# Turning the queries of A and both sides of B's and C's heads through memory, on Trainium2

## The chip, the cores and the metric

The kernel runs on one core of a Trainium2 chip. The metric is the device time of one execution in microseconds (us). TensorE (PE in the profile) multiplies matrices, VectorE (DVE), ScalarE (ACT) and GpSimd (POOL) work on tiles in the core's memory (SBUF; VectorE and ScalarE also on PSUM, where TensorE writes), and SyncE (SP) issues most of the DMAs. Each engine works through its own instructions in order and waits on semaphores.

## The reference, cut to what matters

Two layers of a decoder trunk over 256 tokens of width 1024, all in float32. Each layer is a feed-forward half step, a mixer, and another feed-forward half step. The mixer projects the tokens once and splits the result among three groups of attention heads of width 64:

```python
proj = u @ w_in
aq = apply_rope(rms_norm(aq, a_q_norm), cos, sin)       # A: 4 query heads
ak = apply_rope(rms_norm(ak, a_k_norm), cos, sin)       #    1 shared key head
o_a = dsa_attention(aq, ak, av, iq, ik, iw)             #    keys chosen per query by an indexer, top 64
bq = apply_rope(rms_norm(bq, b_q_norm), cos, sin)       # B: 4 heads, one causal block of 256
bk = apply_rope(rms_norm(bk, b_k_norm), cos, sin)
o_b = moba_attention(bq, bk, bv)
cq, ck = rms_norm(cq, c_q_norm), rms_norm(ck, c_k_norm) # C: 8 heads, no rotation
log_f = log_sigmoid(cf + forget_bias)
o_c = forgetting_attention(cq, ck, cv, log_f) * sigmoid(cg)
return concat([o_a, o_b, o_c]) @ w_out
```

Scores are products over the 64 columns of a head. TensorE sums over partitions, so queries and keys, which the projection leaves with tokens in partitions, have to be turned: columns of two heads to 128 partitions, tokens along the row.

## The kernel before

**Weights.** All weights stream through once. A raw piece of 512 KB is loaded by SP (`Weights.issue`, `load`, L214) into one of ten buffers, ScalarE rounds it (`high`, L273, tile `wh`) and VectorE takes the rest (`low`, L277, tile `wl`), into one of eight pairs; TensorE multiplies with both parts (L383). `W.pump` makes the next pair. `W.hold` stops new loads, `W.free` lets them go on.

**The mixer** (`mixer`). The projection goes over 32 weight units; a unit is a *step*: twelve matmuls, then `run_side`, then a pump. The chunks come in this order: the indexer's queries and small things with B's queries (steps 1 to 8), B's keys and values (9 to 12), A (13 to 16), C's keys (17 to 20), C's queries (21 to 24), C's values (25 to 28), C's gate (29 to 32). After a chunk's last unit its `post_` function empties PSUM and books later work with `at_step(number, fn)`; `run_side` issues what is due at the end of a step, in order of the numbers. So an instruction's place on each engine is set by such numbers, and the engines run as far ahead as their waits let them.

**Turning.** `pairs_T` (L986, L988) turns a pair of heads by transposes on TensorE into a PSUM bank, which ScalarE copies: `bq_turn` and `bk_turn` at step 18.83, `a_turn` at 26.29. C's 16 transposes come after step 32 in `c_T` (L1444, L1445), one pair of heads of queries and keys each, into the tile `spare`. The kernel has another way already, for the feed-forward's hidden tiles, the gate and one pair of probabilities: `to_memory` transposes 32x32 blocks on VectorE (L474, STREAM_TRANSPOSE) and writes them to DRAM (L475), `from_memory` reads them back in four DMAs (L479), so that the blocks come out in their places. `blocks` joins the two.

**Norms.** The heads' norm factors come from ScalarE's squares, VectorE's sums (L963) and a power on GpSimd (`rsqrt`, L394); GpSimd multiplies by them (`scale_heads`, L955), rotates (`rope`, L947 to L950) and applies C's gains `gc` (L1236). `c_norm` does both sides of C at step 25.36.

**Attention.** `run_heads` gives functions for scores, masks (m), exponentials (e), divisions (d on VectorE, D on ScalarE) and flips (f: the transposes of the probabilities on TensorE, L1318). B's are booked by step. After step 32, `AC_ORDER` lists the words for A's heads (0 to 3) and C's (4 to 11) with the output projection's halves (q) among them; `s` are scores of a pair of heads, `g` is `c_T`, `a` adds the causal mask to a pair of C's forget rows on GpSimd (L1145). So m0, e0, D0, f0 are the first head of A. A's mask `amask` is made on VectorE (L1099 to L1103) after the last pass of the top-8 selection (L1092, L1094). C's forget rows are written to DRAM by ScalarE's queue and spread over the partitions from there (`mask_tiles` at step 29.63).

Of the kernel before, what the change touches and what calls it, by code (L numbers as in the profile page):

```python
# [18 lines left out]
P = 128  # L19
S = 256  # L20
# [19 lines left out]
g2.4 g0.5 s0.01 m0 s1.23 m3 e0 e3 s2.45 D0 q g1.0 a0 m4 m2 e2 q q D3 f0.3 a1 a3 m1 e1 s3.42 s4.01 f3.3  # L40
m5 e4 a2 m6 d2 q g3.5 d1 f2.3 q e5 m7 f1.5 m8 D4 s5.32 t m10 v0.0 w o0 e10 q q q e6 f4.3 q d5 m11 d10
# [5 lines left out]
B_TURN, A_ROPE, B_STEP, A_ROOT, A_TURN, SUMS_STEP, MASK_STEP = 18.83, 19.48, 20.73, 23.66, 26.29, 22.33, 29.63  # L47
# [248 lines left out]
def kernel(ctx: ExitStack, tc: tile.TileContext, x, xt, weights, small, const, out):  # L296
# [625 lines left out]
    def mixer(l, norm, nxt):  # L922
        room = wide().rearrange("p (n h d) -> p n h d", n=4, h=8)
# [90 lines left out]
        def post_ib(ps):  # L1014
# [132 lines left out]
        def post_a(ps):  # L1147
# [80 lines left out]

        def post_ck(ps):
            c_sums(0, ck, ps, 20.76)  # L1230

        def post_cq(ps):
            c_sums(1, cq, ps, 24.83)
            for t in range(2):
                q = cq[t]
                G.tensor_tensor(q, q, gc[:, None, :].to_broadcast([P, 8, HD]), op=ALU.mult)  # L1236

            def c_norm():
                rs = head_rs(c_ss.rearrange("p i t h -> p (i t h)"), 32, "c")
                for t in range(2):  # L1240
                    for i, d in enumerate((ck, cq)):
                        x = d[t]
                        scale_heads(x, x, rs[:, 16 * i + 8 * t:16 * i + 8 * t + 8])

            at_step(25.36, c_norm)
# [20 lines left out]
        def run_heads(hs, qk, take, emit=None):
            pj, pt, op, sums, bs = {}, {}, {}, {}, {}

            def scores(i):

                kind, h = hs[i]
                if h % 2:
                    return
                q, k = qk(kind, h)
                bs[i], bs[i + 1] = take(), take()
                for cols, qs, ks in ((slice(0, P), slice(0, P), slice(0, P)),
                                     (slice(P, 3 * P), slice(P, S), slice(0, S))):
                    products((bs[i], bs[i + 1]), cols, q[:, qs], k[:, ks], cols.start == 0)
# [45 lines left out]
            def flip_pair(i):  # L1324

                d = tab.rearrange("p a b t d -> p (a b t d)")[:, :6 * P]
                blocks([pj.pop(2 * i + e) for e in range(2)], 3, "pd", d.rearrange("p (i x) -> p i x", i=8))
# [98 lines left out]
        cT = st["cT"]  # L1426

# [11 lines left out]
        def c_T(j, copy):  # L1439

            b = take()
            for c, src in enumerate((cq, ck)):
                for t in range(2):
                    T.transpose(b[:, c * S + t * P:c * S + (t + 1) * P], src[t][:, 2 * j:2 * j + 2], ident)  # L1444
            copy(cT[:, j], b.rearrange("p (c s) -> p c s", c=2))  # L1445

        def blocks(tiles, n, name, to):
            sc = memory(n, name)
            for t, x in enumerate(tiles):
                to_memory(sc, t, x, n)  # L1450
            from_memory(sc, to, nc.sync)

        def turn_gate(_):
            blocks(st["gate"], 4, "gd", st["sg"].rearrange("p i m r -> p i (m r)"))

        def qk_ac(kind, h):
            if kind == "A":
                return st["aqT"][:, h // 2], st["akT"][:, 0]
            return cT[:, h // 2, 0], cT[:, h // 2, 1]
# [3 lines left out]
        run = dict(q=lambda i: next(halves), w=lambda i: W.pump(), m=masks, e=exps, d=divide, D=lambda i: divide(i, True),  # L1463
                   T=flip_pair, t=turn_gate,
                   s=lambda i: scores(2 * i), f=flip, F=lambda i: flip(i, V.tensor_copy),
                   g=lambda i: c_T(i, A.copy), G=lambda i: c_T(i, V.tensor_copy),
# [70 lines left out]
```

## Time and profile before

| | us |
|---|---|
| median of 3 runs (lowest to highest) | 975.02 (974.76 to 975.63) |
| the profiled execution | 974.23 |
| its span, first to last instruction | 972.5 |
| TensorE busy in the span | 967.3 |
| VectorE busy in the span | 822.5 |
| ScalarE busy in the span | 611.1 |
| GpSimd busy in the span | 167.2 |

Names such as `ps_gu<-wh,xhl` are the tile written and the tiles read. A duration of a matmul includes its way through the array, so rows of matmuls overlap; what one costs on the path is read from the chain or from the starts of its neighbours. "[0.50 <-PE ps_gu L383]" at a row's end says that the engine sat idle for 0.50 us before it, until TensorE's write.

### The profile page before, as it was taken

To read this page: it belongs to the slowest core of one execution; us is meant where nothing else is said; L and a number is where in the kernel's file an instruction comes from. 1 tells how busy PE (TensorE), PEld (TensorE's weight loads), DVE (VectorE), ACT (ScalarE), POOL (GpSimd) and SP (SyncE) were. 2 spreads that over 40 slices of the span, in tenths; PEclk is the share of its full clock that TensorE was granted. 3 is DMA by queue.
4 is the path that set the end of the run, shared out by engine and by line. 5 is a ranking of instruction groups with operands and counts; after the bars stand their busy time and mean duration, and the time that the engine had idled before them with its cause. 6 is when DMAs were issued, how large, how long until landed. Compare 5 with 4: busy or idle time off the path is not lost.

```text
span 972.5 us, 13771 instructions
## 1 busy us (share of the span) xinstructions
PE 967.3 (99%) x4608; PEld 801.1 (82%) x4608; DVE 822.5 (85%) x1284; ACT 611.1 (63%) x1024; POOL 167.2 (17%) x190
## 2 busy tenths in 40 slices
PE   9999999999999999999999999999999999999998
PEld 8888888888878888888878888888888788888887
DVE  6999698789987799879679987977899877998794
ACT  7756574567876656537475654756677966575562
POOL 0000002187630000000000000031867200000000
PEclk9999999999999999999999999999999999999999
DMA  9878877685555686769587777867657447687661
GB/s 360 309 198 335 281 257 217 210 295 170 184 183 161 249 229 240 268 193 315 174 322 267 209 248 246 289 197 255 245 160 232 167 147 268 186 304 265 183 243 65
DMA packets 105495, 226.68 MB, mean 233 GB/s; under 512 B 20928, under 2 KB 50896, under 8 KB 105424
## 3 DMA queue, kind: packets, MB, share of 16 engines
q1 hardware_dynamic: 101936, 213.95, 63.2%
q0 software_dynamic: 2304, 8.39, 4.9%
q10 hardware_dynamic: 1184, 3.46, 1.1%
q8 instruction: 36, 0.59, 0.2%
q14 instruction: 35, 0.29, 0.1%
HBM read 208.44 MB, written 17.33 MB: 232 GB/s over the span
## 4 chain that ended last, share of the span: by engine, by line
PE 97%; DMA 2%; DVE 1%; SPq 0%; ACT 0%; issue 0%; POOL 0%; ACTq 0%; POOLq 0%
PE ps_gu L383 65%; PE ps_acc L383 29%; PE ps_gu L1318 1%; PE ps_acc L986 1%; DMA xd<-tmp 1%; PE ps_acc L418 0%; DMA hd<-tmp 0%; DMA hT<-hd 0%; PE ps_acc L1318 0%; DMA xT<-xd 0%; PE ps_acc L1444 0%; SPq L479 0%; DVE tmp L474 0%; DVE trunk L490 0%; DVE wl L277 0%
## 5 line engine op out<-in xcount | busy, mean ns | idle before, releaser
L383 PE MATMUL ps_gu<-wh,xhl 128*128 128x512 f32 (+2 forms) x1600 | 493.7, 386 | 0.6 <-ACT xhl L447 0.6
L277 DVE TENSOR_TENSOR wl<-raw,wh 128x1024 fp32r<-128x1024 f32 (+2 forms) x340 | 405.1, 1228 | 13.4 <-ACT wh L273 13.3
L273 ACT CAST wh<-raw 128x1024 fp32r<-128x1024 f32 (+2 forms) x340 | 340.0, 1040 | 55.1 <-PE ps_gu L383 16.9
L383 PEld LDWEIGHTS ps_gu<-wh,xhl 128*128 128x128 f32 x1600 | 298.8, 188 | 59.3 <-ACT xhl L447 1.1
L383 PE MATMUL ps_gu<-wl,xhl 128*128 128x512 f32 (+2 forms) x800 | 305.9, 384 | 0.0
L383 PEld LDWEIGHTS ps_gu<-wl,xhl 128*128 128x128 f32 x800 | 150.3, 188 | 28.1
L383 PE MATMUL ps_acc<-wh,hh 128*128 128x512 f32 (+1 forms) x352 | 136.8, 389 | 0.2 <-ACT hh L567 0.2
L383 PE MATMUL ps_acc<-wh,hl 128*128 128x512 f32 (+1 forms) x352 | 136.7, 388 | 0.0
L383 PE MATMUL ps_acc<-wl,hh 128*128 128x512 f32 (+1 forms) x352 | 136.4, 387 | 0.0
L273 ACT CAST wh<-wide 128x1024 fp32r<-128x1024 f32 x48 | 50.2, 1054 | 85.7 <-DVE wide L244 55.1
L242 POOL DMA_DIRECT2D raw<-in_weights_dram x16 | 14.3, 893 | 377.3 <-DVE wide L244 256.0
L383 PEld LDWEIGHTS ps_acc<-wh,hl 128*128 128x128 f32 x352 | 66.1, 188 | 14.7 <-DVE hl L568 1.4
L383 PEld LDWEIGHTS ps_acc<-wh,hh 128*128 128x128 f32 x352 | 66.1, 188 | 14.0 <-ACT hh L567 0.9
L383 PEld LDWEIGHTS ps_acc<-wl,hh 128*128 128x128 f32 x352 | 66.1, 188 | 13.5
L277 DVE TENSOR_TENSOR wl<-wide,wh 128x1024 fp32r<-128x1024 f32 x48 | 57.8, 1212 | 3.5 <-ACT wh L273 3.2
L567 ACT CAST hh<-hT 128x256 fp32r<-128x256 f32 x88 | 29.4, 405 | 41.8 <-DMA hT<-hd 41.8
L568 DVE TENSOR_TENSOR hl<-hT,hh 128x256 fp32r<-128x256 f32 x88 | 31.9, 422 | 20.8 <-ACT hh L567 20.8
L555 DVE SCALAR_TENSOR_TENSOR tmp<-ps_gu,y_n,tmp 128x512 f32<-128x512 f32 (+1 forms) x32 | 21.3, 667 | 29.6 <-PE ps_gu L383 27.4
L394 POOL TENSOR_TENSOR y_n<-msq,minus_half 128x2 f32<-128x2 f32 x6 | 8.6, 1437 | 199.8 <-DVE msq L393 199.8
L244 DVE TENSOR_TENSOR wide<-wide,raw 128x1024 f32<-128x1024 f32 x32 | 39.1, 1221 | 0.6
L474 DVE STREAM_TRANSPOSE tmp<-tmp 128x512 f32<-128x512 f32 (+1 forms) x52 | 34.6, 669 | 1.7
L551 ACT ACTIVATE tmp<-tmp,y_n 128x512 f32<-128x512 f32 x16 | 11.5, 721 | 35.1 <-DVE tmp L681 35.1
(259 smaller groups left out, 1116.8 us busy)
## 6 DMA issues: line engine op xcount, KB each, us to landing
raw<-in_weights_dram SPq DMA_DIRECT2D x324, 512.0 KB, 5.3
hd<-tmp SPq DMA_DIRECT2D x40, 256.0 KB, 2.0
hT<-hd SPq DMA_DIRECT2D x80, 128.0 KB, 2.6
raw<-in_weights_dram POOLq DMA_DIRECT2D x16, 512.0 KB, 6.6
raw<-in_weights_dram SPq DMA_DIRECT2D x8, 384.0 KB, 6.2
raw<-in_weights_dram SPq DMA_DIRECT2D x8, 336.0 KB, 3.6
raw<-in_weights_dram SPq DMA_DIRECT2D x8, 256.0 KB, 4.4
fmask<-fd ACTq DMA_DIRECT2D x2, 768.0 KB, 6.9
```

The source lines that it names most:

```text
L242: self.nc.gpsimd.dma_start(self.part(*unit), self.kept(rs[0], *unit[1:]), accum_op=ALU.add)
L244: self.nc.vector.tensor_tensor(self.part(*unit), *(self.part(r, *unit[1:]) for r in rs), op=ALU.add)
L273: self.nc.scalar.copy(hv, src)
L277: (engine or self.nc.vector).tensor_tensor(lv, self.srcs[self.n_low], hv.bitcast(F32), op=ALU.subtract)
L383: T.matmul(o, l, r, start=start, stop=stop, skip_group_check=True)
L474: V.transpose(o.rearrange("p (j b c) -> p b j c", j=4, b=n), x.rearrange("p (b j c) -> p b j c", b=n, j=4))
L551: A.activation(a, ps[t][:, :n], AF.Silu, scale=norm.r[:, t:t + 1])
L555: V.scalar_tensor_tensor(a, u, norm.r[:, t:t + 1], a, op0=ALU.mult, op1=ALU.mult)
L567: A.copy(by(hh), x)
L568: V.tensor_tensor(by(hl), x, by(hh).bitcast(F32), op=ALU.subtract)
L986: T.transpose(ps[:, i * S + t * P:i * S + (t + 1) * P], xs[t][:, (j + i) * P:(j + i + 1) * P], ident)
L1318: T.transpose(b[:, j * P:(j + 1) * P], pj[i][:, j * P:(j + 1) * P], ident)
```

## The change

The queries of A and both sides of B and C are no longer turned on TensorE; `blocks`, now `turned`, takes them through memory. Queries are the stationary side of the scores and are copied once more on ScalarE into rows without gaps (`bq_whole`, `aq_whole`, `c_pairs`); the keys of B and C are read as they lie, in runs of 32 tokens. Only A's single key head stays on TensorE. The turned tiles lie in the tiles `wide` and `tab` and in the place of B's keys. C's norm is split: gains and factors go to the keys, behind A's rotation at step 21, and the queries' factors to step 25; their trips through memory stand at steps 25 and 28, and weight loads are held between. The spreading of the forget rows moves from step 30 to 25, past B's scores. `AC_ORDER` loses two of its four `g` words.

```diff
-g2.4 g0.5 s0.01 m0 s1.23 m3 e0 e3 s2.45 D0 q g1.0 a0 m4 m2 e2 q q D3 f0.3 a1 a3 m1 e1 s3.42 s4.01 f3.3
-m5 e4 a2 m6 d2 q g3.5 d1 f2.3 q e5 m7 f1.5 m8 D4 s5.32 t m10 v0.0 w o0 e10 q q q e6 f4.3 q d5 m11 d10
+g0 s0.01 m0 s1.23 m3 e0 e3 s2.45 D0 q g1 a0 m4 m2 e2 q q D3 f0.3 a1 a3 m1 e1 s3.42 s4.01 f3.3
+m5 e4 a2 m6 d2 q d1 f2.3 q e5 m7 f1.5 m8 D4 s5.32 t m10 v0.0 w o0 e10 q q q e6 f4.3 q d5 m11 d10
...
-B_TURN, A_ROPE, B_STEP, A_ROOT, A_TURN, SUMS_STEP, MASK_STEP = 18.83, 19.48, 20.73, 23.66, 26.29, 22.33, 29.63
+A_ROPE, B_STEP, A_ROOT, SUMS_STEP, MASK_STEP = 19.48, 20.73, 23.66, 22.33, 24.5
...
+    def turned(tiles, n, name, to):
+        sc = memory(n, name)
+        for t, x in enumerate(tiles):
+            to_memory(sc, t, x, n)
+        from_memory(sc, to, nc.sync)
...
             def bq_turn():
+                to = wide_room[:, :512].rearrange("p (i x) -> p i x", i=8)
+                turned(rot, 2, "bqd", to)
+                st["bq"] = to.rearrange("p i (m r) -> p m i r", m=2)
+
+            def bq_whole():
                 st["bqT"] = at.tile([P, 2, S], F32, name="bqT", tag="qs")
-                pairs_T(st["bqT"], rot)
-
-            at_step(B_TURN, bq_turn)
+                A.copy(st["bqT"].rearrange("p m (i r) -> p m i r", i=8), st["bq"])
+
+            at_step(13.0, bq_turn)
+            at_step(18.0, bq_whole)
...
-            def a_turn():
+            def aq_turn():
+                to = tab.rearrange("p a b t d -> p (a b t d)")[:, :512].rearrange("p (i x) -> p i x", i=8)
+                turned(rot, 2, "aqd", to)
+                st["aq"] = to.rearrange("p i (m r) -> p m i r", m=2)
...
+            def aq_whole():
                 st["aqT"] = at.tile([P, 2, S], F32, name="aqT", tag="qs")
-                st["akT"] = at.tile([P, 1, S], F32, name="akT", tag="ikT")
-                pairs_T(st["aqT"], rot)
-                pairs_T(st["akT"], [d.rearrange("p a b -> p (a b)") for d in akd])
-
-            at_step(A_TURN, a_turn)
+                A.copy(st["aqT"].rearrange("p m (i r) -> p m i r", i=8), st["aq"])
+
+            at_step(20.95, aq_turn)
+            at_step(26.29, ak_turn)
+            at_step(26.29, aq_whole)
...
-                st["bkT"] = at.tile([P, 2, S], F32, name="bkT", tag="kT")
-                pairs_T(st["bkT"], rot)
+                to = at.tile([P, 512], F32, name="bkT", tag="kT").rearrange("p (i x) -> p i x", i=8)
+                turned(rot, 2, "bkd", to)
+                st["bkT"] = to.rearrange("p i (m r) -> p m i r", m=2)
...
-            at_step(B_TURN, bk_turn)
+            at_step(14.7, bk_turn)
...
+            at_step(20.9, gains)
+            at_step(21.0, lambda: c_norm(0, ck, "ck"))
+            at_step(24.9, lambda: st.update(ckT=c_turn(1, ck, "kd")))
...
-            at_step(25.36, c_norm)
+            at_step(24.84, lambda: c_norm(1, cq, "cq"))
+            at_step(24.45, lambda: setattr(W, "hold", True))
+            at_step(27.9, lambda: st.update(cqT=c_turn(0, cq, "qd")))
+            at_step(27.9, lambda: W.free(2))
```

What that does to the engines' orders, in layer 1. First VectorE around the end of C's queries (steps 25 to 28): c_ss are the sums of squares of C's heads, `wl` weight splits, `m` the top-8 selection, `wide` the tile that holds C's queries and keys. Before:

```order
L963 TENSOR_REDUCE c_ss<-tmp 128x8 x2
L277 TENSOR_TENSOR wl<-raw,wh 128x1024
L393 TENSOR_SCALAR c_ss<-c_ss 128x32
L277 TENSOR_TENSOR wl<-raw,wh 128x1024
L1092 MAX m_2741<-score_2109 128x8
L1092 MAX m_2742<-score_2110 128x8
L1094 MATCH_REPLACE score_2109<-m_2741,score_2109 128x128
L1094 MATCH_REPLACE score_2110<-m_2742,score_2110 128x256
L277 TENSOR_TENSOR wl<-raw,wh 128x1024 x2
```

After:

```order
L970 TENSOR_REDUCE c_ss<-tmp 128x8 x2
L393 TENSOR_SCALAR c_ss<-c_ss 128x16
L474 STREAM_TRANSPOSE tmp<-wide 128x4x4x32 x2
L277 TENSOR_TENSOR wl<-raw,wh 128x1024 x2
L1105 MAX m_2772<-score_2109 128x8
L1105 MAX m_2773<-score_2110 128x8
L1107 MATCH_REPLACE score_2109<-m_2772,score_2109 128x128
L1107 MATCH_REPLACE score_2110<-m_2773,score_2110 128x256
L277 TENSOR_TENSOR wl<-raw,wh 128x1024
L474 STREAM_TRANSPOSE tmp<-wide 128x4x4x32 x2
L277 TENSOR_TENSOR wl<-raw,wh 128x1024
```

The keys' block transposes stand behind the sums, the queries' one split later than the top-8 pass. GpSimd from A's last rotation on, `y_` being the norm factors and `fmask`, `spare`, `gmask` the forget rows with the causal mask to be added. Before:

```order
L950 TENSOR_TENSOR ak_2333<-ak_2333,swapped 128x64
L394 TENSOR_TENSOR y_a<-ssa,minus_half 128x10
L955 TENSOR_TENSOR akd_2334<-ak_2332,y_a 128x128
L955 TENSOR_TENSOR akd_2335<-ak_2333,y_a 128x128
L970 TENSOR_SCALAR minus_a<-y_a 128x10
L1236 TENSOR_TENSOR wide<-wide,gc 128x512 x2
L394 TENSOR_TENSOR y_c<-c_ss,minus_half 128x32
L955 TENSOR_TENSOR wide<-wide,y_c 128x512 x4
L1145 TENSOR_TENSOR fmask<-fmask,causal 128x2x2x128 x2
```

After:

```order
L957 TENSOR_TENSOR ak_2356<-ak_2356,swapped 128x64
L1268 TENSOR_TENSOR wide<-wide,gc 128x512 x2
L394 TENSOR_TENSOR y_ck<-c_ss,minus_half 128x16
L962 TENSOR_TENSOR wide<-wide,y_ck 128x512 x2
L394 TENSOR_TENSOR y_a<-ssa,minus_half 128x10
L962 TENSOR_TENSOR akd_2357<-ak_2355,y_a 128x128
L962 TENSOR_TENSOR akd_2358<-ak_2356,y_a 128x128
L977 TENSOR_SCALAR minus_a<-y_a 128x10
L394 TENSOR_TENSOR y_cq<-c_ss,minus_half 128x16
L962 TENSOR_TENSOR wide<-wide,y_cq 128x512 x2
L1158 TENSOR_TENSOR fmask<-fmask,causal 128x2x2x128 x2
```

Half of C's norm now stands ahead of A's factors, in a place where GpSimd had nothing to do. Last, TensorE at A's and C's first scores after step 32 (`wide` on its left is C's queries and keys, `ident` the unit matrix of a transpose). Before:

```order
L1444 MATMUL ps_acc<-ident,wide 128x128 x8
L383 MATMUL ps_gu<-akT,aqT 128x128 x2
L383 MATMUL ps_gu<-akT,aqT 128x256 x2
L383 MATMUL ps_gu<-akT,aqT 128x128 x2
L383 MATMUL ps_gu<-akT,aqT 128x256 x2
L383 MATMUL ps_acc<-spare 128x128 x2
```

After:

```order
L383 MATMUL ps_gu<-akT,aqT 128x128 x2
L383 MATMUL ps_gu<-akT,aqT 128x256 x2
L383 MATMUL ps_gu<-akT,aqT 128x128 x2
L383 MATMUL ps_gu<-akT,aqT 128x256 x2
L383 MATMUL ps_acc<-wide,spare 128x128 x2
```

The eight transposes ahead of A's scores are gone, and C's scores read their keys from `wide`.

## Rows read from the trace of the kernel before

**Rows 1.** The profile's page, part 1: busy time (share) x instructions of each engine.

```profile
PE 967.3 (99%) x4608; PEld 801.1 (82%) x4608; DVE 822.5 (85%) x1284; ACT 611.1 (63%) x1024; POOL 167.2 (17%) x190
```

**Rows 2.** Waits of TensorE: waiter <- releaser: us in total, times, longest.

```profile
PE ps_gu L383 <- POOL minus_half L336: 1.0, 1, 1.0
...
```

**Rows 3.** The chain in order of time, 225 to 310 us: start, us, what.

```profile
231.92 0.87 PE ps_acc L986 x8
...
257.72 0.65 PE ps_acc L986 x6
...
274.36 0.87 PE ps_acc L1444 x8
...
278.29 0.44 PE ps_gu L1444 x4
```

**Rows 4.** Stretches: us, busy of each engine (instructions), PEclk, DMA, GB/s.

```profile
244.00:276.00 32.00, 32.00 (x173) 26.18 (x173) 31.51 (x74) 23.23 (x46) 21.20 (x13) 1.00 0.65 223
...
726.00:758.00 32.00, 32.00 (x170) 26.15 (x170) 31.79 (x76) 23.21 (x48) 21.21 (x13) 1.00 0.66 220
```

**Rows 5.** Timeline of VectorE, two places: start, us, instruction, count [idle before].

```profile
171.71 0.45 DVE L474 STREAM_TRANSPOSE tmp<-trunk 128x256 f32<-128x256 f32 x1
...
284.59 1.28 DVE L474 STREAM_TRANSPOSE tmp<-tmp 128x512 f32<-128x512 f32 x2
```

**Rows 6.** Timeline of VectorE, 241 to 277 us, up to m0.

```profile
241.24 0.69 DVE L963 TENSOR_REDUCE c_ss<-tmp 128x8 f32<-128x512 f32 x1 [0.55 <-ACT tmp L959]
...
256.87 1.43 DVE L277 TENSOR_TENSOR wl<-raw,wh 128x1024 fp32r<-128x1024 f32 x1
...
265.87 1.73 DVE L277 TENSOR_TENSOR wl<-raw,wh 128x1024 fp32r<-128x1024 f32 x1
...
268.70 1.89 DVE L277 TENSOR_TENSOR wl<-raw,wh 128x1024 fp32r<-128x1024 f32 x1
270.51 1.06 DVE L1099 TENSOR_SCALAR amask<-score 128x128 f32<-128x128 f32 x1
271.50 2.69 DVE L1101 SCALAR_TENSOR_TENSOR amask<-score,cst 128x128 f32<-128x128 f32 x2
...
274.50 1.22 DVE L277 TENSOR_TENSOR wl<-raw,wh 128x1024 fp32r<-128x1024 f32 x1
276.22 0.35 DVE L1292 CUSTOM_DVE_ANT_0 tmp<-ps_gu,amask,minus_a 128x128 f32<-128x128 f32 x1 [0.50 <-PE ps_gu L383]
```

**Rows 7.** Timeline of GpSimd, 258 to 274 us.

```profile
258.47 6.37 POOL L394 TENSOR_TENSOR y_c<-c_ss,minus_half 128x32 f32<-128x32 f32 x1 [1.25 <-DVE c_ss L393]
264.92 6.57 POOL L955 TENSOR_TENSOR wide<-wide,y_c 128x512 f32<-128x512 f32 x4
271.45 2.58 POOL L1145 TENSOR_TENSOR fmask<-fmask,causal 128x512 f32<-128x512 f32 x2
```

**Rows 8.** Timelines of ScalarE and TensorE: D0 and f0.

```profile
278.40 0.79 ACT L1311 ACTIVATE p<-p,sums 128x128 f32<-128x128 f32 x2
...
279.95 0.49 PE L1318 MATMUL ps_gu<-ident,p 128*128 128x128 f32 x3
```

**Rows 9.** Timelines of VectorE and TensorE: division and flip of B's last head.

```profile
253.24 0.55 DVE L1313 TENSOR_SCALAR p<-p,sums 128x128 f32<-128x128 f32 x2
...
254.16 0.82 PE L1318 MATMUL ps_acc<-ident,p 128*128 128x128 f32 x6
```

**Rows 10.** Timeline of SyncE's queue: the gate's reads from memory.

```profile
288.88 1.80 SPq L479 DMA_DIRECT2D spare<-gd  x4
```

**Rows 11.** DMA issues: out<-in, engine, count, KB each, median us to landing.

```profile
xd<-tmp SPq DMA_DIRECT2D x10, 128.0 KB, 1.7
xT<-xd SPq DMA_DIRECT2D x20, 64.0 KB, 2.0
...
hd<-tmp SPq DMA_DIRECT2D x8, 128.0 KB, 3.9
```

**Rows 12.** Timelines of VectorE and TensorE: splits after step 13, and B's scores.

```profile
226.81 4.08 DVE L277 TENSOR_TENSOR wl<-raw,wh 128x1024 fp32r<-128x1024 f32 x3
...
235.46 1.58 PE L383 MATMUL ps_acc<-bkT,bqT 64*128 64x128 f32 x16
```

More of the change, by code (lines that the diff above doesn't have):

```diff
@@ L1227, in c_sums, with c_norm, c_turn, gains @@
             at_step(when, sums)
+        def c_norm(i, d, tag):
+            rs = head_rs(c_ss[:, i].rearrange("p t h -> p (t h)"), 16, tag)
+            for t in range(2):
+                scale_heads(d[t], d[t], rs[:, 8 * t:8 * t + 8])
+        def c_turn(i, d, name):
+            to = wide_room[:, 1024 * i:1024 * i + 1024].rearrange("p (i x) -> p i x", i=8)
+            turned([x.rearrange("p h d -> p (h d)") for x in d], 4, name, to)
+            return to.rearrange("p i (m r) -> p m i r", m=4)
         def post_ck(ps):
             c_sums(0, ck, ps, 20.76)
+            def gains():
+                for t in range(2):
+                    k = ck[t]
+                    G.tensor_tensor(k, k, gc[:, None, :].to_broadcast([P, 8, HD]), op=ALU.mult)
+            at_step(20.9, gains)
+            at_step(21.0, lambda: c_norm(0, ck, "ck"))
+            at_step(24.9, lambda: st.update(ckT=c_turn(1, ck, "kd")))
         def post_cq(ps):
             c_sums(1, cq, ps, 24.83)
[L1234 to L1243, printed above, removed]
-            at_step(25.36, c_norm)
+            at_step(24.84, lambda: c_norm(1, cq, "cq"))
+            at_step(24.45, lambda: setattr(W, "hold", True))
+            at_step(27.9, lambda: st.update(cqT=c_turn(0, cq, "qd")))
+            at_step(27.9, lambda: W.free(2))
         hr = sm.tile([P, 2], F32, name="hr", tag="hr")
@@ L1275, in scores @@
                 bs[i], bs[i + 1] = take(), take()
-                for cols, qs, ks in ((slice(0, P), slice(0, P), slice(0, P)),
-                                     (slice(P, 3 * P), slice(P, S), slice(0, S))):
-                    products((bs[i], bs[i + 1]), cols, q[:, qs], k[:, ks], cols.start == 0)
+                for cols, qs, n in ((slice(0, P), slice(0, P), P), (slice(P, 3 * P), slice(P, S), S)):
+                    some = k[:, :n] if len(k.shape) == 2 else k[:, :n // 32]
+                    products((bs[i], bs[i + 1]), cols, q[:, qs], some, cols.start == 0)
             def masks(i):
@@ L1326, in flip_pair @@
                 d = tab.rearrange("p a b t d -> p (a b t d)")[:, :6 * P]
-                blocks([pj.pop(2 * i + e) for e in range(2)], 3, "pd", d.rearrange("p (i x) -> p i x", i=8))
+                turned([pj.pop(2 * i + e) for e in range(2)], 3, "pd", d.rearrange("p (i x) -> p i x", i=8))
                 d = d.rearrange("p (e i b c) -> p e i b c", e=2, i=4, b=3)
@@ L1437, in take, with c_pairs @@
             return banks[i]
[L1439 to L1451, printed above, removed]
+        c_q = st["cq"]
+        def c_pairs(j):
+            two = slice(2 * j, 2 * j + 2)
+            A.copy(c_q[:, two].rearrange("p m (i r) -> p m i r", i=8), st["cqT"][:, two])
         def turn_gate(_):
-            blocks(st["gate"], 4, "gd", st["sg"].rearrange("p i m r -> p i (m r)"))
+            turned(st["gate"], 4, "gd", st["sg"].rearrange("p i m r -> p i (m r)"))
         def qk_ac(kind, h):
@@ L1458, in qk_ac @@
                 return st["aqT"][:, h // 2], st["akT"][:, 0]
-            return cT[:, h // 2, 0], cT[:, h // 2, 1]
+            return c_q[:, h // 2], st["ckT"][:, h // 2]
         hs = [("A", h) for h in range(4)] + [("C", h) for h in range(8)]
         scores, masks, exps, divide, flip, flip_pair, values, outT = run_heads(hs, qk_ac, take)
-        run = dict(q=lambda i: next(halves), w=lambda i: W.pump(), m=masks, e=exps, d=divide, D=lambda i: divide(i, True),
+        run = dict(q=lambda i: next(halves), w=lambda i: W.pump(), m=masks, e=exps, d=divide, D=lambda i: divide(i, True), g=c_pairs,
                    T=flip_pair, t=turn_gate,
                    s=lambda i: scores(2 * i), f=flip, F=lambda i: flip(i, V.tensor_copy),
-                   g=lambda i: c_T(i, A.copy), G=lambda i: c_T(i, V.tensor_copy),
                    v=lambda i: values(2 * i + 1),
```

9 lines of the change are left out of this document (6 added, 3 removed).

## The prediction

> **What bounds the kernel now.** I read the page first: TensorE is busy 967.3 of 972.5 us [rows 1]. The view of waits names three for it in the whole run, the longest the 1.0 us before its first product [rows 2]. So a matmul that is taken away shortens the run by its share of the chain, unless the place it leaves is filled with waiting. The chain in order of time shows what the transposes on TensorE cost there: 0.87 us for the eight of B (queries and keys), 0.65 for six of A, of which four are queries (0.43), 0.87 for the first eight of C and 0.44 for the next four; another four stand at 283.12 in the same way [rows 3]. Then the view of stretches, for who is next: from 244 to 276 us VectorE is busy 31.51 of 32.00 us [rows 4]. Layer 2 repeats layer 1 about 482 us later (31.79 of 32.00 from 726 to 758), so I work on layer 1 and double.
>
> **What it removes.** 0.87 + 0.43 + 0.87 + 0.44 + 0.44 = 3.05 us of TensorE in a layer, 6.1 us in both. The Trainium skill would price it lower: "TensorE: Matmul & The Clock Gate", section "Wait — 56ns, not 53.3ns?", has a warm 128-column matmul every 55.6 ns, so 28 of them 1.6 us a layer and 3.1 in place of 6.1 in both; these rows give 0.11 us each, and the rows decide. ScalarE loses three of its eight copies of turned tiles; it is not last in any step below.
>
> **What it adds on VectorE.** Each turned tile costs a 32x32 block transpose there. Two of 128x512 took 1.28 us, one of 128x256 0.45 [rows 5]. Per layer: queries and keys of B 0.8 each, queries of A 0.8, keys and queries of C 1.3 each: 5.0 us, on an engine without idle time. I follow it to the place where TensorE first needs the result, the transposes of A's first probabilities.
>
> B's 1.6 us are spent before 243.7. VectorE waits there for ScalarE, as the 0.55 us before the sums of C's keys at 241.24 [rows 6] and two more pauses of that size show, and those absorb the addition. I carry 0 (-0.3 to +0.4).
>
> From 243.7 to the first masked score of A (m0): A's queries 0.8, the extra small scale of c_ss 0.1, C's keys 1.3, C's queries 1.3: +3.5.
>
> **What it gives back there.** The three instructions that start A's mask at 270.51 and 271.50, and the one after them, last until 274.50: 4.0 us for three 128x128 tiles and one of 128x384 [rows 6]. GpSimd is at work under them: its four scales end at 271.5 and its two causal adds run from 271.45 to 274.03 [rows 7], and the vector instructions end with those. The weight splits of 1.73 and 1.89 us stand under the same scales, and the one at 274.50, which stands alone, takes 1.22 [rows 6]. The change takes half of GpSimd's work on C to step 21, where its power function needs 16 columns instead of 32 (6.37 us now [rows 7]; I take about 3, between half of it and less). Queries of C are then scaled by 265, the causal adds done by 268, and the mask at about 275 meets an idle GpSimd. Two such instructions of 128x128 and 128x256 take 0.55 together in a division [rows 9], so I take 0.3 for each of the four: 4.0 becomes 1.2, -2.8. The two splits give 1.2 and the one of 1.43 at 256.87 [rows 6], under the gains of C that move too, 0.2: -4.2 in all.
>
> GpSimd's moved instructions meet others: three pairs (scales of keys, scales of queries, causal adds), each over one weight split or so, at the 0.5 that the 1.73 row shows over 1.22: +1.5 (0 to 2). And C's query transposes wait for GpSimd. VectorE arrives there at 256.9 + 0.9 + 0.5 (a met split) + 1.3 (keys) + three splits of 1.2 and a pass of the top-8 of 1.2 = 264.4, or 0.3 later; GpSimd, from its c_ss at 258.5, is there after the power function (2.6 to 3.2) and two scales of 1.3 to 1.6 at 263.7 to 265.0. I take 0.1 (0 to 0.5), near the middle. What is queued behind that wait is splits, and those are steps ahead of TensorE: no split is among its waits [rows 2].
>
> So VectorE ends its last split before m0 at 275.72 + 3.5 - 4.2 + 1.5 + 0.1 = 276.6. Now m0 starts at 276.22 after 0.50 us of waiting for TensorE [rows 6], so +0.4.
>
> **Where TensorE meets it.** m0 is followed by the exponentials and the division on ScalarE, which ends at 279.19; TensorE transposes that tile at 279.95 [rows 8]. Shifted by 0.4 it is there at 279.6, and with 0.1 of signalling TensorE goes on at 279.7: 0.25 us earlier than now. It would have come earlier, but waits: first for the last head of B, whose division ends at 253.8 and whose transposes stand at 254.16 [rows 9]. With 0.9 for A's queries and c_ss, and 0.5 for the keys' scales, that tile comes at 255.2, one us late; A's 0.43, C's 0.87 and 0.44 are gained after that, so TensorE reaches f0 at 279.2 and waits 0.5. After f0 the four transposes at 283.12 are gone: -0.44. Masks of C wait for TensorE there, so both go along. Result per layer: -0.25 - 0.44 = -0.7; two layers: -1.4.
>
> **The queues it passes.** Both sides of B and the others go out and back on SP, two writes and four reads each. SP's reads of a turned tile take 1.80 us to issue [rows 10]; a write of 128 KB landed in 1.7 or 3.9 us, a read of 64 KB in 2.0 [rows 11]. B's keys are the tight ones. VectorE's block of three splits at 226.81 [rows 12] now has their transposes behind its first split: 226.8 + 0.2 + 1.2 = 228.2, ready 229.0, write issued 229.3 and landed 231.0, reads issued by 232.8, landed 234.8. The scores stand at 235.46 [rows 12], without the eight transposes at 234.6: a wait of 0.2, which the wait for B's last head swallows. With the 3.9 us write it is 237.0. C's queries: transposes from 265 to 266.3, written by 269.2, read by 271.0, landed by 273.6; their copy stands on ScalarE behind the gate's tanh, later than that. Weight loads stop for three steps (about 8 us) and on SP behind those reads; ten buffers of weights are full ahead of a use that slows down after step 32, so I put that at nothing; if the cover were gone, it is a wait of TensorE for splits, which the trace of before doesn't have. The masks' rows go out on ScalarE's queue five steps earlier: two issues, and their target is free when B's scores are done. Keys of B and C are read with runs of 32 elements; no row of another cost is seen for such reads, 0.
>
> **The rivals.**
> - Forecast, 0.48: as worked out, 975.02 - 1.4 = 973.6 (the profiled execution took 974.23, 1.7 of it outside its span of 972.5, and would come to 972.8; the median lies 0.8 above it). About 0.2%, 2 us, is what a measurement of this kernel can tell from no change.
> - GpSimd's moved instructions meet no split, 0.30. Then VectorE carries 3.5 - 4.2 = -0.7 to m0 and TensorE is held by B's last head alone: ready at 253.8 + 0.9 + 0.1 = 254.8, +0.65; then -0.43 - 0.87 - 0.44 = -1.09 at f0, -0.44 after: -1.53, two layers -3.1: 971.9. For it: no split under GpSimd's power function is delayed, though several stand there. Against: 1.73 and 1.89 [rows 6].
> - VectorE holds nothing up, 0.07: all 6.1 us are gained, 968.9. Against it: 31.51 of 32.00 us.
> - Slower: the relief at A's mask doesn't come, 0.08. If GpSimd reaches its causal adds as late as now (after about 270, for a late landing of the masks' rows or a long power function), the 2.8 us stay: m0 at 279.4, +3.2; the tile of f0 at 282.4, TensorE +2.5 and -0.44: +2.1 a layer, 979.1. It decides from about 1.7 of the 2.8 us on.
> - Slower: B's keys come late, 0.07. With the 3.9 us write TensorE stands until 237.0, 1.6 later than now; C's key projection, its squares and VectorE follow by 1.6, m0 too, f0 by 1.4, -0.44: +1.0 a layer, 977.0. The Trainium skill speaks for this one ("DMA: Bandwidth & Descriptors", section "Specifications": below 512 B a transfer is a read-modify-write, and these runs are 256 B). Reads of that kind landed in 2.0 us here [rows 11], so the trace shows no such penalty.
>
> **How the numbers follow.** Faster by over 0.2%: 0.30 + 0.07 = 0.37. Within: 0.48. Slower: 0.15. The range leaves out the full gain and the missing relief, and takes the second rival with 1 us for the carry, and B's keys: 970.8 to 977.0. The likeliest case's own, by 0.7 us a layer either way, is 972.2 to 975.0.
>
> **What would show it.** TensorE's waits in the profile after: one before B's last head (about 1 us), one before A's first probabilities (about 0.5), each twice, and a small one before B's scores. Right steps: A's mask in about 1.2 us, GpSimd's causal adds before 270, m0 at about 276.6. Wrong: no TensorE wait at all (then the gain is 6 us), a mask that still takes 4 us, a wait of ScalarE for C's queries, or weight splits that TensorE waits for.

## The result, and the profile after

| | before | after |
|---|---|---|
| median (lowest to highest), us | 975.53 (974.76 to 976.12) | 986.94 (981.94 to 988.85) |
| ratio, 95% interval | | 1.0109 (1.0082 to 1.0135) |
| span of the profiled execution, us | 972.5 | 982.4 |

The change makes the kernel slower by about 11 us, where 973.6 was forecast within 970.8 to 977.0. The five runs after lie 7 us apart, with granted clocks of 0.992 to 1.000, and the one at 1.000 is the shortest. The page, part 1 (as [rows 1]), and TensorE's waits (as [rows 2], where the longest was 1.0 at the start):

```profile
PE 969.2 (99%) x4552; PEld 798.0 (81%) x4552; DVE 831.1 (85%) x1306; ACT 608.9 (62%) x1018; POOL 166.7 (17%) x192
```

```profile
PE ps_gu L383 <- DMA tab<-pd: 2.2, 2, 1.9
PE ps_acc L383 <- DMA bkT<-bkd: 2.2, 2, 1.7
PE ps_acc L383 <- ACT wide L981: 1.9, 1, 1.9
PE ps_acc L1352 <- DVE p L1347: 1.1, 2, 1.0
...
PE ps_gu L1352 <- DVE p L1347: 0.5, 1, 0.5
```

56 matmuls fewer, and yet TensorE is busy for 1.9 us more. So there are two things to look for: waits (some 8 us with the start left out), and work that takes longer.

**B's keys.** The wait of 1.9 is the first score of B in layer 1, those of 1.7 and 0.4 the same place in layer 2. That the first names ScalarE's tile `wide` misleads: that tile is C's keys, which happened to be written at 237.57; B's queries, the only thing the scores need of ScalarE, had been copied by 228.3. What the scores wait for are the reads of B's keys. VectorE, SyncE's queue and TensorE, layer 1 (as [rows 12]):

```profile
229.69 0.76 DVE L474 STREAM_TRANSPOSE tmp<-bkr 128x256 f32<-128x256 f32 x2
```

```profile
230.24 0.90 SPq L475 DMA_DIRECT2D bkd<-tmp  x2
234.86 1.80 SPq L479 DMA_DIRECT2D bkT<-bkd  x4
```

```profile
237.64 3.58 PE L383 MATMUL ps_acc<-bkT,bqT 64*128 64x128 f32 x16 [1.93 <-ACT wide L981]
```

Between the second write (230.7) and the first read SyncE waits 4 us for the write to be seen. The write goes out right behind a load of weights (issued at 229.83), and the bytes of both keep the DMA engines until 234 (106 GB/s from 230 to 232, 274 from 232 to 234, 26 after). And the scores take 3.58 us where they took 1.58. TensorE in stretches (us, busy, clock, DMA share, GB/s):

```profile
234.00:236.00 2.00, 1.71 (x8) 1.00 0.09 26
236.00:238.00 2.00, 0.36 (x2) 0.92 0.86 142
238.00:240.00 2.00, 2.00 (x13) 0.50 0.70 260
240.00:242.00 2.00, 2.00 (x10) 0.72 0.99 401
242.00:244.00 2.00, 2.00 (x11) 1.00 1.04 414
```

The clock fell to 0.50, its lower level of 1.2 GHz, at the end of the wait, and was back by 242. In layer 2 of this execution it stayed at 1.00. Waits included, this place is 3.98 us longer than before in layer 1 and 2.63 in layer 2, so by the difference the half clock cost some 1.35 us in this execution (an estimate).

**A's stage.** VectorE and GpSimd there (as [rows 6] and [rows 7]; A's mask, m0, and the divisions of A's heads 2 and 1):

```profile
276.38 0.22 DVE L1112 TENSOR_SCALAR amask<-score 128x128 f32<-128x128 f32 x1
276.51 0.48 DVE L1114 SCALAR_TENSOR_TENSOR amask<-score,cst 128x128 f32<-128x128 f32 x2
...
278.96 0.35 DVE L1326 CUSTOM_DVE_ANT_0 tmp<-ps_gu,amask,minus_a 128x128 f32<-128x128 f32 x1 [0.43 <-PE ps_gu L383]
...
284.88 1.58 DVE L1347 TENSOR_SCALAR p<-p,sums 128x128 f32<-128x128 f32 x2
...
286.57 1.38 DVE L1347 TENSOR_SCALAR p<-p,sums 128x128 f32<-128x128 f32 x2
```

```profile
266.60 4.61 POOL L1158 TENSOR_TENSOR fmask<-fmask,causal 128x512 f32<-128x512 f32 x2
284.94 1.37 POOL L1158 TENSOR_TENSOR spare<-spare,causal 128x512 f32<-128x512 f32 x1 [13.73 <-DMA spare<-fd]
286.27 1.33 POOL L1158 TENSOR_TENSOR gmask<-gmask,causal 128x512 f32<-128x512 f32 x1
```

The mask takes 1.0 us (4.0 before) and m0 waits for TensorE. But the two divisions, 0.55 us each before, take 1.58 and 1.38, under two causal adds of GpSimd that ran from 278.1 to 280.7 before (this is layer 1; in layer 2 they take 0.55 and 2.42). GpSimd waited 13.7 us for the last forget rows, and gmask's add stood behind that. The flips waiting for these divisions are the waits of 0.5 (layer 1) and 1.0 (layer 2). DMA issues (KB each, median us to landing):

```profile
spare<-fd ACTq DMA_DIRECT2D x2, 384.0 KB, 6.9
pd<-tmp SPq DMA_DIRECT2D x4, 192.0 KB, 5.1
...
bqd<-tmp SPq DMA_DIRECT2D x4, 128.0 KB, 2.7
...
bkd<-tmp SPq DMA_DIRECT2D x4, 128.0 KB, 4.2
bkT<-bkd SPq DMA_DIRECT2D x8, 64.0 KB, 2.0
aqd<-tmp SPq DMA_DIRECT2D x4, 128.0 KB, 2.3
```

Before, the forget rows (`spare<-fd`) landed in 3.6 us, the pair of probabilities (`pd`) in 2.5. The waits for `tab<-pd`, 0.3 and 1.9, follow from the last.

### The profile page after: what moved, and what is told of

It is laid out like the page before. It is cut to its first block, busy times and chain, and to the rows that moved or that the text cites. A ratio compares the mean times of both kernels' runs of the same rounds, so it can differ in the third digit from the quotient of the medians.

```text
span 982.4 us, 13788 instructions
## 1 busy us (share of the span) xinstructions
PE 969.2 (99%) x4552; PEld 798.0 (81%) x4552; DVE 831.1 (85%) x1306; ACT 608.9 (62%) x1018; POOL 166.7 (17%) x192
## 4 chain that ended last, share of the span: by engine, by line
PE 89%; DVE 5%; DMA 3%; ACT 2%; issue 1%; SPq 0%; DVEq 0%; POOL 0%; ACTq 0%; POOLq 0%
PE ps_gu L383 60%; PE ps_acc L383 28%; DVE wl L277 1%; DMA pd<-tmp 1%; DVE score L1091 1%; DVE p L1347 1%; DMA raw<-in_weights_dram 1%; DMA xd<-tmp 1%; DVE tmp L474 0%; DMA tab<-pd 0%; PE ps_acc L418 0%; PE ps_acc L1352 0%; SPq L479 0%; DVE tmp L1326 0%; ACT wh L273 0%
## 5 line engine op out<-in xcount | busy, mean ns | idle before, releaser
L383 PEld LDWEIGHTS ps_acc<-wh,hl 128*128 128x128 f32 x352 | 66.1, 188 | 14.2 <-DVE hl L574 0.5
L1335 ACT ACTIVATE p<-tmp,nm 128x128 f32<-128x128 f32 x64 | 28.5, 449 | 12.0 <-DVE nm L1326 11.0
```

Of the source, the lines that this page charges most:

```text
L383: T.matmul(o, l, r, start=start, stop=stop, skip_group_check=True)
L1335: A.activation(p[:, c], s[:, c], AF.Exp, bias=nm[:, t:t + 1], scale=-1.0, accum_out=sums[i][:, t:t + 1])
```

## The experiments

| run | median, us | ratio to before (95%) |
|---|---|---|
| e1_bkeys_pe | 979.41 | 1.0039 (1.0023 to 1.0056) |
| e2_no_hold | 996.95 | 1.0236 (1.0200 to 1.0271) |
| e3_bkeys_only | 978.00 | 1.0027 (1.0013 to 1.0041) |
| e4_b_later | 992.29 | 1.0175 (1.0155 to 1.0195) |
| e5_before_shifted | 977.06 | 1.0020 (1.0010 to 1.0030) |
| e6_swap | 975.32 | 1.0010 (1.0000 to 1.0021) |
| e7_a_pe | 974.96 | 1.0008 (0.9994 to 1.0021) |
| e8_filled | 982.39 | 1.0079 (1.0064 to 1.0094) |
| e9_v4_first | 972.78 | 0.9979 (0.9968 to 0.9991) |
| e10_best | 972.70 | 0.9976 (0.9966 to 0.9986) |
| e11_before_mended | 974.59 | 0.9995 (0.9985 to 1.0004) |
| e12_held_long | 987.21 | 1.0130 (1.0113 to 1.0147) |

The kernel before had medians of 973.95 to 975.40 beside them.

### B's keys back on TensorE, and alone through memory

```diff
-                to = at.tile([P, 512], F32, name="bkT", tag="kT").rearrange("p (i x) -> p i x", i=8)
-                turned(rot, 2, "bkd", to)
-                st["bkT"] = to.rearrange("p i (m r) -> p m i r", m=2)
+                st["bkT"] = at.tile([P, 2, S], F32, name="bkT", tag="kT")
+                pairs_T(st["bkT"], rot)
...
-            at_step(14.7, bk_turn)
+            at_step(18.83, bk_turn)
```

> The changed kernel, with the keys of B alone turned on TensorE again. Theory (B's keys come too late through memory): TensorE's waits before B's scores (1.9 us in layer 1, 1.7 and 0.4 in layer 2) and the half clock behind them go; the step of the projection that holds those scores, 3.98 and 2.63 us dearer in the changed kernel than before, is at most 0.2 dearer; the granted clock is 1.00 in every run; a layer pays 0.44 for four transposes. Time about 977 (975.5 to 979.5), with the runs no more than 2 us apart. Rival (VectorE is the bound, and the wait for B's keys only stands where its delay is first seen): what is won before B's scores comes back as longer waits before B's last head and before A's first probabilities, and the time stays above 983.

7.5 us less by the medians (6.8 by the ratios), though TensorE has eight transposes more. The scores wait for nothing and take 1.51 us. But the clock still slipped to 0.999 in the profiled run, the runs lie 3.3 us apart where at most 2 was expected, and the time is 2 us above the theory's figure: part of the rival holds. Waits of TensorE:

```profile
PE ps_acc L1351 <- DVE p L1346: 2.7, 5, 1.0
...
PE ps_gu L1351 <- DVE p L1346: 0.5, 1, 0.5
PE ps_gu L383 <- DMA tab<-pd: 0.3, 1, 0.3
```

Of these, 0.72 + 0.16 and 0.75 + 0.15 stand before B's last head, where they were forecast, 0.5 before A's third flip in layer 1 and 1.0 before its fourth in layer 2, as after the change. The counterpart is the kernel before with this one part of the change, and the scores reading such keys:

```diff
-                st["bkT"] = at.tile([P, 2, S], F32, name="bkT", tag="kT")
-                pairs_T(st["bkT"], rot)
+                to = at.tile([P, 512], F32, name="bkT", tag="kT").rearrange("p (i x) -> p i x", i=8)
+                turned(rot, 2, "bkd", to)
+                st["bkT"] = to.rearrange("p i (m r) -> p m i r", m=2)
...
-            at_step(B_TURN, bk_turn)
+            at_step(14.7, bk_turn)
```

> The kernel before, with the keys of B alone turned through memory at step 14.7 and read as in the changed kernel. Theory (B's keys are late by themselves, since a write takes near 4 us to be seen): TensorE waits 1 to 2 us before B's scores in each layer, the clock falls behind some of these waits, and four transposes (0.44 us) a layer are saved: 977 to 983. Rival (they are late only because the rest of the change, queries of B on VectorE and GpSimd's earlier work among it, is in front of them): no wait of 0.3 us or more before B's scores, 974 to 975.

Two waits of 0.8, so the keys are late by themselves, and 2.6 us of time; the granted clock was 1.00 in the profiled run and 0.998 in the two longest. The theory asked for waits of 1 to 2 us: with the whole change they are 1.9 and 2.1, so the rest of it adds 1.1 to 1.3. The scores behind the wait also take longer, 2.0 us for 1.5, at full clock. Wait and scores make the place 1.30 and 1.43 us longer in the two layers, 0.44 each is saved, and so the trace gives 1.9 of the 2.6.

```profile
PE ps_acc L383 <- DMA bkT<-bkd: 1.6, 2, 0.8
```

### What the clock costs

```diff
                 bs[i], bs[i + 1] = take(), take()
+                for _ in range(9 if kind == "B" and i == 2 else 0):
+                    mm(bs[i][:, :P], ones, ones, True, True)
```

> The changed kernel with nine matmuls of 128 columns on constants (0.21 us each, 1.9 us) put on TensorE just before B's first scores, where it waits for B's keys; their result is overwritten. Theory (the clock falls for the waiting): the scores start at the same time, 237.6, TensorE hardly waits there, the granted clock is 1.00 in every run, B's scores take 1.5 us (3.5 in layer 1 of the changed kernel), and the runs come together near 982 (980.5 to 983.5). Rival (the clock falls for something else, or what it costs is small): clock and spread of the runs as in the changed kernel, 982 to 989, or all of them above 985 since the added matmuls cost 1.9 us a layer.

The theory holds: all four runs have clock 1.00 and lie from 981.7 to 983.4. Work added to TensorE made the kernel 4.5 us shorter by the medians (2.9 by the ratios). They lie where the changed kernel's own run with clock 1.000 lies (981.94), so what the filling takes away is the clock; the wait itself stays. Timeline and stretches of TensorE (18 records are nine matmuls):

```profile
236.16 2.17 PE L383 MATMUL ps_acc<-ones 128*128 128x128 f32 x18
238.26 0.49 PE L383 MATMUL ps_acc<-bkT,bqT 64*128 64x128 f32 x2
238.94 1.54 PE L383 MATMUL ps_acc<-bkT,bqT 64*128 64x128 f32 x14 [0.20 <-DMA bkT<-bkd]
```

```profile
238.00:240.00 2.00, 1.80 (x18) 1.00 0.79 178
```

### B's attention a step later, and no stop of the weight loads

```diff
-A_ROPE, B_STEP, A_ROOT, SUMS_STEP, MASK_STEP = 19.48, 20.73, 23.66, 22.33, 24.5
+A_ROPE, B_STEP, A_ROOT, SUMS_STEP, MASK_STEP = 19.48, 21.73, 23.66, 22.33, 24.5
```

> The changed kernel with all of B's attention booked one step (2.7 us) later, and nothing else changed. Theory (late keys): the scores then stand at about 238, when the keys are there (237.6 in the changed kernel): no wait, clock 1.00, all transposes still saved. Waits further on (0.5 to 1 before A's second flips, 0.3 to 1.9 for the pair of probabilities) stay: 976 (974 to 979). Rival (VectorE is the bound): B's divisions come one step later and with them its last flips; B's last head waits, A's mask and its first probabilities are later by what B was moved, and the time stays above 982.

The rival holds. The scores stand at 239.0 without a wait, but B's last division falls behind sums and transposes of C and under GpSimd (2.20 us at 262.58, in place of 0.55), and its flips wait 5.1 us in each layer, with the clock at 0.50 for 4 us behind the first of these waits:

```profile
PE ps_acc L1352 <- DVE p L1347: 11.2, 4, 5.1
```

VectorE has no room to take B's attention later. The other edit:

```diff
-            at_step(24.45, lambda: setattr(W, "hold", True))
...
-            at_step(27.9, lambda: W.free(2))
```

> The changed kernel without the stop of weight loads from step 25 to 28. Theory (the loads that were held go out together afterwards and slow the last forget rows and the probabilities that go through memory): the rows of the tile spare land less than 5 us after their issue (6.8 in the changed kernel, 3.7 before), GpSimd's two causal adds end before VectorE's divisions of A (0.55 us each again, not 1.6 and 1.4), and TensorE's waits before those flips (0.5 and 1.0) and for the turned pair of probabilities (0.3 and 1.9) are gone: 3 to 4 us, 983 (981 to 985, the wait for B's keys and its clock staying). Rival (the stop protects C's trips through memory): SP's writes and reads of C's queries stand behind loads that wait for buffers, ScalarE's copy of them comes late, TensorE waits 2 us or more before C's scores, and the time is 988 or above.

The rival again, in its wait and its time. TensorE waits twice, 5.2 and 5.5 us, before C's first scores, for ScalarE's copy of C's queries (`spare`). Their reads do not stand behind loads in SyncE's order, as the rival has it; their write does, and it is seen late: 7.3 us from the first write to the first read (9.3 in layer 2), where the changed kernel has 3.2 (268.77 to 271.98) and 4.0.

```profile
PE ps_acc L383 <- ACT spare L1473: 10.7, 2, 5.5
```

```profile
269.39 1.33 SPq L214 DMA_DIRECT2D raw<-in_weights_dram  x3
270.78 1.21 SPq L475 DMA_DIRECT2D qd<-tmp  x2
278.06 1.80 SPq L479 DMA_DIRECT2D wide<-qd  x4
```

The theory's part came too: the last forget rows landed in 4.3 us and the divisions took 0.55 each, but TensorE was 5 us late by then. So the stop is needed; what it costs is another matter, below.

### Where the tiles lie

Splitting C's norm made two tiles of 128 bytes of factors (`y_ck`, `y_cq`) where there was one (`y_c`). Every tile behind it in SBUF moved 128 bytes on; those of which the feed-forward keeps its sums (`fp` and others, stationary in 384 matmuls) began at multiples of 256 bytes before (the first `fp` at byte 213760 of its partition in the built kernel, 213888 after). In the traces after, those matmuls start 234 ns apart, before 227. Alone:

```diff
-        y = sm.tile([P, 32], F32, name="y_" + tag, tag="y_" + tag, bufs=1)[:, :n]
+        y = sm.tile([P, 64 if tag == "c" else 32], F32, name="y_" + tag, tag="y_" + tag, bufs=1)[:, :n]
```

> The kernel before with one small tile (the norm factors of C) 128 bytes longer, so that every tile behind it in SBUF lies 128 bytes further, as in the changed kernel, where a second such tile does it. Nothing else differs. Theory: the matmuls of the feed-forward whose stationary tiles (fp, fpT, fva0, fva1, fqs, fg) lie there take 234 ns each in place of 227 in every kernel of this family and 227 in the two with the layout of before; 384 of them, 2.8 us: 978.2 (977 to 979), and the pace of wh,fp reads 234. Rival (the pace has another cause in the changed kernel): 227 and 975.4.

The pace is 234, and the time 1.7 us longer (interval 1.0 to 2.9). Groups of matmuls (count | busy, mean ns | idle), with the shift, and then before:

```profile
L383 PE MATMUL ps_gu<-wh,fp 128*128 128x512 f32 x96 | 34.1, 396 | 0.0
```

```profile
L383 PE MATMUL ps_gu<-wh,fp 128*128 128x512 f32 x96 | 33.4, 389 | 0.0
```

The forecast of 2.8 took 7.3 ns for all 384; not all of the groups slow down as much (fp on `wh` by 7.4, fpT by 3.7 ns), and by groups it comes to 2.3 or 2.4. The tiles that move through the array there (`wh`, `wl`) lie ahead of the longer tile and kept their places, and the groups whose stationary tiles do too (`xhl`, `hh`, `hl`) kept their pace, so it is the place of the stationary tile that counts. Only this one shift was run.

### GpSimd's adds, and A's queries

On top of B's keys on TensorE, with `[P, 16 if n == 16 else 32]` for the factor tiles (places as before):

```diff
-... D3 f0.3 a1 a3 m1 e1 ... m5 e4 a2 m6 ...
+... D3 f0.3 a1 a2 m1 e1 ... m5 e4 a3 m6 ...
```

> The changed kernel with B's keys on TensorE, the tiles back in the places of before (the two factor tiles of C half as long), and the causal add of gmask ahead of that of spare on GpSimd. Theory: the places give 2.8 us back; the first add is done before 272 and only the add of spare still meets a division of A (one of about 1.4 us, the other 0.55 again), so of TensorE's waits before A's flips (0.5 us in layer 1, 1.0 in layer 2) at most 0.5 is left in each: 979.4 - 2.8 - 0.6 = 976.0 (975 to 977). Rival (the divisions are long for another reason than GpSimd's adds): both divisions stay at 1.4 to 1.6 us and the time is 976.6 or more.

As the theory has it: 4.1 us less than without the two edits (2.8 by the ratios), one wait of 0.50 left in each layer before A's flips, put down to ScalarE's copy of turned probabilities (`pT`). The divisions take 0.55 and 0.81 in layer 1; in layer 2 one still takes 1.57. Next, A's queries turned on TensorE as before, the other edits kept:

```diff
-            at_step(20.95, aq_turn)
-            at_step(26.29, ak_turn)
-            at_step(26.29, aq_whole)
+            at_step(26.29, a_turn)
```

> The same with the queries of A on TensorE too, so that only queries of B and both sides of C go through memory. Theory (VectorE's 0.8 us of transposes of A are what makes B's last head late): TensorE's wait there (0.72 and 0.16 us with A through memory) falls below 0.2, a layer pays 0.43 for four transposes, and the time is 0.4 to 1 us below the run with A through memory: about 975 (974 to 976). Rival (it is late for the division that meets GpSimd's scales of C's keys, 1.13 us in place of 0.35): 0.5 us or more of the wait stay, and the time is equal or higher.

The wait before B's last head falls from 0.69 + 0.15 to 0.15, as the theory says. But from the first of the six flips there to the next weights it is still 1.00 us (0.57 before), and the time did not follow (ratio 1.0008 for 1.0010): in the profiled run the pair of probabilities cost 2.0 and 0.7 us.

### The pair of probabilities

```diff
-o3 v5.1 v4.3 o4 w q q
+o3 v4.3 o4 v5.1 w q q
```

> The kernel with only B's queries and both sides of C through memory, tiles in the places of before, gmask's add first, and now the values of heads 8 and 9 of C ahead of those of 10 and 11 (whose probabilities go through memory). Theory: TensorE's wait for the turned pair of probabilities (2.0 and 0.7 us) shrinks by the eight matmuls that go ahead, 0.65 us each time: 975.0 - 1.3 = 973.7 (972.8 to 974.8). Rival (other work is late behind it, the output of head pair 4 or the last sums): no gain, 975.

2.2 us less by the medians (2.8 by the ratios), which is more than the 1.3 expected; one wait of 1.2 us was left in the profiled run. Then the load taken from beside the pair (`h` sets W.hold, `l` is W.free(2)):

```diff
-... s5.32 t m10 ... v1.3 T5 o1 ...
+... s5.32 h t m10 ... v1.3 T5 l o1 ...
```

> The same, and weight loads stopped from the gate's trip through memory to behind the reads of that pair, which moves one load of 512 KB behind four reads in each layer. Theory (the pair's second write is seen late, after 3.3 to 6.1 us in place of 2.6, for the load that runs beside it): the write is seen within 3 us, no wait of TensorE above 0.3 for the pair, 972.7 (971.5 to 973.8), below the kernel before. Rival (the write is slow for the rest of the traffic, or the load that was moved is missed by the next feed-forward): the wait stays, or TensorE waits for splits after 316; 973.7 or more.

By the trace the theory holds: the reads are issued 2.8 us after the first write, and TensorE waits for nothing there. SyncE's queue in e7_a_pe, then here:

```profile
290.26 0.38 SPq L214 DMA_DIRECT2D raw<-in_weights_dram  x1
291.25 1.24 SPq L475 DMA_DIRECT2D pd<-tmp  x2
297.07 1.80 SPq L479 DMA_DIRECT2D tab<-pd  x4
```

```profile
292.05 1.25 SPq L475 DMA_DIRECT2D pd<-tmp  x2
294.88 1.96 SPq L479 DMA_DIRECT2D tab<-pd  x4
```

The time is that of e9_v4_first (972.70 after 972.78), so what this edit alone is worth can't be told. This is the version that beats both kernels, by 0.24% over the kernel before. Control, these two edits on the kernel before:

> The kernel before with these same two edits and nothing else: values of heads 8 and 9 first, weight loads stopped during the pair's trip. Theory (the kernel before has no wait there, 0 in its trace): no change, 975.4 (974.6 to 976.0), so that what the run beside it gains is owed to the turning of C and of B's queries. Rival (the edits help by themselves): 974.4 or less.

No change that can be told (0.9995, its interval holds 1), so most of the gain is owed to the turning.

### Why the forget rows are late

```diff
-            at_step(27.9, lambda: W.free(2))
...
-... s5.32 h t m10 ...
+... s5.32 t m10 ...
```

> The run with weight loads stopped during the pair's trip, with that stop made one with the earlier one: no load goes out between C's keys and the reads of the pair, so the eight loads that stood between C's queries and the gate come after the pair. Theory (the rows of spare land late for those loads): the rows land within 4 us of their issue (5.3 to 6.9 us before this edit, 3.6 in the kernel before), GpSimd's add of spare ends before VectorE's second division of A, which takes 0.55 us again (1.25); since that division hid behind other work in the run without this edit, the gain is 0 to 0.3 us, if the loads, now all at once after 297, do not meet the next norm's trip through memory at 311 to 319. If they do, TensorE waits there (0.7 to 3 us in each layer). 972.3 to 976. Rival (the rows are late for another reason, the order on ScalarE's queue or GpSimd): they still take 5 us or more.

The theory holds for the rows: landed 3.4 us after their issue, the add over before the divisions, which take 0.55 each. Timeline of GpSimd:

```profile
279.84 1.29 POOL L1158 TENSOR_TENSOR spare<-spare,causal 128x512 f32<-128x512 f32 x1 [9.41 <-DMA spare<-fd]
```

The time was missed, by a mechanism neither theory had: ScalarE's next rounding of weights waits 5.8 us for its load, and the cast of a head pair's output (`oh`), which TensorE needs, stands behind it in ScalarE's order. The two waits of TensorE, one a layer, make 10.5 us, and behind the first the clock was 0.51 from 300 to 304 and 0.64 from 304 to 308; the two together are most of the 14.5 us over e10_best.

```profile
301.38 1.04 ACT L273 CAST wh<-raw 128x1024 fp32r<-128x1024 f32 x1 [5.77 <-DMA raw<-in_weights_dram]
302.33 0.40 ACT L1384 CAST oh<-o 128x256 fp32r<-128x256 f32 x1
```

```profile
302.78 0.79 PE L383 MATMUL ps_acc<-wh,oh 128*128 128x512 f32 x1 [4.99 <-ACT oh L1384]
```

## Why the prediction was wrong, by its steps

- **What it removes:** right. The places of B, A and C's next four are 0.88, 0.40 to 0.44 and 0.44 us shorter, the rows' prices. C's first eight gave 0.69 for 0.87, since the scores beside them went from 2.17 to 2.35 us: their pairs of matmuls, 6 ns apart before, start up to 90 ns apart. B's scores did the same in e3_bkeys_only. Why is open. That keys are now read in runs of 32, which the prediction put at nothing, isn't it by itself, for scores of C's third group take 1.03 us in the changed kernel and 0.86 in e8_filled, which reads them alike.
- **B's keys:** this is the step that failed, in the term of the write. The text had 1.7 and 3.9 us in [rows 11] and took 1.7 for the forecast; 4.2 was measured. Writes of the same form for B's and A's queries were seen in 2.7 and 2.3, so it is not the form. What sets B's keys apart is the load of weights right ahead of the write, in both layers and in every run that turns them through memory (landed in 3.9 to 4.2); the writes of the queries had none in the 2.5 us before them. The same holds in e2_no_hold (7.3 us for 3.2, C's queries) and, the other way, in e10_best (2.8 for 5.8, the pair of probabilities). No run takes the load from before B's keys, so for them this is likely and not shown. The Trainium skill, "Perfetto Trace Analysis", section "DMA Instruction — HWDGE (DVE, Sync)", says that the semaphore's update waits until the write is complete, which can take surprisingly long when the target is HBM; here the write took 4.2 us and the read from there 2.0, but other writes of 128 KB only 1.7 to 2.7, so the target alone does not make it long. VectorE's transposes also came 1.5 us later than worked out, most of that with a profiled execution that runs about 1.1 us behind by then.
- **The rival "B's keys come late":** the right mechanism with 0.07 and too low a price. It moved TensorE by 1.6 us a layer and left out the clock, which e8_filled puts at 2.9 to 4.5 us for the run, and the spread of the runs. The penalty for short runs that was cited for it isn't seen: the reads landed in 2.0 us.
- **B's last head, one us late:** right once the keys are on time (0.88 and 0.90 in e1_bkeys_pe); A's transposes on VectorE are most of it (0.15 in e7_a_pe).
- **VectorE up to m0:** right, in part by luck. The mask takes 1.0 (forecast 1.2), and in e1_bkeys_pe m0 is at 276.6, the forecast's value; but that execution ran 0.45 us behind at the place that was 243.67 before (244.12), and from there VectorE took 32.34 us for 32.05: 0.3 more, where 0.9 was forecast. The second rival, that GpSimd's moved work meets no split, did not hold either: under it stand a split of 1.89 us at 265.82 and a division of 1.34 at 251.92. GpSimd's adds ended at 271.2 (forecast 268; in e1_bkeys_pe 269.2), ahead of the mask. The wait of 0.5 before A's first flip did not come, since TensorE was late itself.
- **"Weight loads stop for three steps; I put that at nothing":** wrong. The prediction asked only whether weights would run out, which they did not. Let go, eight loads go out together (DMA share 1.0 from 278 to 286) beside the last forget rows, and e12_held_long shows the rows' 3.4 us without them. The rows hold GpSimd, its adds then meet divisions that had met none. The Trainium skill, "SBUF — State Buffer", section "SBUF: two separate sides", has an exclusive lock on the port pair that VectorE and GpSimd share, held for a whole instruction; the trace agrees (1.58 and 1.38 for 0.55, over 0.15 and 0.35 us after the adds end, and 0.55 again in e12_held_long).
- **Not in the prediction at all:** the 128 bytes, 1.7 us, which no list of instructions shows.

Taken away in turn, with 14.2 us between the medians of the change (986.94) and of e10_best (972.70): B's keys with their clock 7.5, tile places and the adds' order 4.1, A's queries and the pair of probabilities 2.6 (by the ratios 6.8, 2.8 and 3.3). What is left of the idea, queries of B and both sides of C on VectorE, removes 4.4 us of transposes (0.44 + 1.75 a layer). By the trace of e10_best some 0.9 of that go to dearer scores and flips of A and C, 1.2 to the place of B's last flips (0.62 a layer) and 0.2 to a wait; that leaves some 2.0, and 2.3 were measured (974.96 to 972.70).

## What to carry to other kernels

When work moves from a full engine into a trip through memory, price the trip by its slowest write in the trace, not its median, look at what its queue sends out just ahead of that write, and ask for each wait it may cause on TensorE what the clock does behind it: here that cost, by e8_filled, 2.9 to 4.5 us beside some 4 us of waits. A stop of loads moves traffic rather than removing it; look at what else is in flight when it ends, and at what stands behind a late load in the order of the engine that uses it. And compare the places of tiles when a small buffer is added, for it moves all that lie behind it.

## What the runs showed of the hardware

- Stationary tiles 128 bytes further: 234 ns in place of 227 from one 512-column matmul to the next, in every kernel with that layout.
- Writes right behind a load of weights on the same queue were seen late: 7.3 us from the first write to the first read for 3.2 (C's queries, e2_no_hold and the change), 5.8 for 2.8 (the pair of probabilities, e7_a_pe and e10_best).
- After a wait of 1.9 us the clock was at 0.50 in layer 1, after 1.7 + 0.4 in layer 2 at 1.00, in one execution; nine matmuls on constants in the wait keep it at 1.00.
- Masks that read PSUM kept their 0.35 us under GpSimd's adds in the kernel before (from 278.1 to 280.7); divisions from SBUF to SBUF grew from 0.55 to 1.58 in the change, and to 2.42 in its layer 2.
